# A hybrid decoder step: cached-row compression moved into sample attention, token preparation first

## The chip, the core and the metric

The kernel runs on one core of a Trainium2 chip. Its engines are TensorE (PE, with PEld for its weight loads), VectorE (DVE), ScalarE (ACT), GpSimd (POOL) and SyncE (SP, which issues the plain DMAs). The metric is device time in microseconds of one launch, as the median of the runs; less is better. All data are float32. Dense products are made from values split into a high and a low part (fp32r), in three matmuls: high x high, high weight rest x high, high x low rest.

## The reference, cut to what matters

One layer serves 512 prompt tokens and 8 sample sequences of 4 tokens each, 544 tokens in all, with the same weights. A wide projection `zin = norm(x) @ w_in` feeds three branches, and a merge and an output projection follow. The change concerns branch A (sparse attention) for the sample tokens. Each of these sequences has 2048 cached rows, in 16 pages of 128 rows; a row has the kinds k_cmp, v_cmp, k_slc, v_slc, each of 2 groups x 128 values. The rows of the first two kinds are compressed, 32 rows (16 new, 16 shared with the next block) to one, 127 blocks per sequence:

```python
blocks = jnp.concatenate([chunks[:, j:j + n_cmp] for j in range(r)], axis=2)
blocks = blocks + jnp.transpose(cmp_pe, (1, 0, 2))[:, :, None, :]
kv_c = jnp.einsum('bilcgd,clde->bicge', blocks, cmp_w.reshape(2, CMP_LEN, HEAD_DIM, HEAD_DIM))
k_c, v_c = kv_c[:, :, 0], kv_c[:, :, 1]
...
sc = jnp.einsum('bqgrd,bigd->bqgri', qb, k_c) * scale
pc = _masked_softmax(sc, (cmp_end[None, :] <= t[:, None])[None, :, None, None, :])
o_cmp = jnp.einsum('bqgri,bigd->bqgrd', pc, v_c)
imp = jnp.einsum('bqgri,ij->bqgj', pc, overlap)
```

`imp` picks the 16 blocks of 64 cached rows that the selected attention reads; the window attention reads the last 512 rows. The three results are weighted by gates and added.

## The kernel before, in words

`run` (line 1728 on) sets the order. First comes **phase_c** (L319), a stage of its own. For each of 8 sequences and 16 row positions `dma(n)` lets POOL gather a tile `pg` (128 partitions x 512 values: key and value of 128 rows) by the row numbers in `idx`; PE transposes it four times into `pT`; ACT and DVE make the high and low parts `sh` and `sl`; and `mms(n)` runs 12 matmuls of 256 columns into `cP` against the compression weights (`cwh`, `cwl`). `fin` adds the bias `peb` (the compressed `cmp_pe`) and writes keys to the DRAM tensor `kcd`; values go, transposed, to `vcd`. Beside it, as a side generator, run `params` and `x_prep` (L276): it loads five tiles of token rows (the fifth has the 32 sample tokens), squares, scales and transposes them into `hT`.

Then `open_d` splits `hT` into `hhi` and `hlo`, and **run_units** walks a list of dense units: kv, gate and q columns (84 units), two gate blocks (64), merge columns, pooling, convolution, merge columns, then the branch and output projections; 612 in all. One unit is 4 k-tiles x 3 products x 2 halves = 24 matmuls of 272 columns into `zin`. Its weights are loaded by SP into `wr` six units ahead (a load of 512 KB serves two units) and split three units ahead into `wh` and `wl`.

The rest of the work hangs on this list as generators, the `sides`: after each unit every side makes `rate` steps, a step being the code up to its next yield. The rate is 1, but 1.5 in the first merge columns (units 148 to 244) and 1.7 in the second. `kv_side` compresses the prompt's rows with weights `cw` loaded for it; `attn_p` is the prompt's attention; after it, in the same chain, comes **samp** (L1319). `samp` first reads `kcd` and `vcd` back (`load`, tiles `kc`, `vc`), makes scores `sc`, a softmax, and outputs `oc`, with lags of two steps, in ten steps for four pairs of sequences. Then `samp_group` makes window and selected attention per pair. The cached rows for it (kinds 2 and 3) are gathered by `need()`: a group is eight gathers of 128 partitions x 256 values into four `kr` tiles, and `need(1)` issues as many groups as leave `AHEAD` = 2 waiting behind the one that it returns. A scheduler orders the built program on each engine. All sides take tiles from one pool `u` of 32 SBUF buffers (`s.U`) and one of four PSUM buffers (`s.A`), so a gather waits until the tile that last had its buffer is done.

## Time and profile before

| | us |
|---|---|
| runs: median (lowest, highest) | 2618.25 (2612.72, 2618.82) |
| span of the profiled execution | 2613.4 |
| PE busy | 2527.3 |
| DVE / ACT / POOL busy | 1165.4 / 772.4 / 490.4 |

The profile is of one execution; its own time is known as its span, from the first to the last instruction, and the runs' times stand beside it. A busy PE is a union of overlapping matmuls, so the number of dense matmuls in a stretch, not the busy share, tells how far the list has come. A fp32 matmul that is no transpose has two records in the trace (512 sO for the 256 of the program).

### The profile page before, as it was taken

Reading aid. Unit: us, or ns where it says so; the run is one execution under the profiler, and the core shown is the slowest. Engines: PE = TensorE matmul, PEld = TensorE weight load, DVE = VectorE, ACT = ScalarE, POOL = GpSimd, SP = SyncE. Lnnn points to the kernel's source line nnn. Section 1 sums busy time; section 2 is a strip of 40 time slices with the busy share of each in tenths; the row PEclk is TensorE's granted clock in tenths of the full one; section 3 lists DMA queues with packets and bytes.
Section 4 is the critical chain, followed back from the end, with each engine's and each line's share of the span. In section 5 each row is a group of like instructions: output and inputs, shape, how many; then the busy total and the mean of one; then the engine's idle time right before and its main releaser. Section 6 shows DMA issues by size and latency. Waiting matters only on the chain.

```text
span 2613.4 us, 49213 instructions
## 1 busy us (share of the span) xinstructions
PE 2527.3 (97%) x20311; PEld 2398.1 (92%) x20311; DVE 1165.4 (45%) x2360; ACT 772.4 (30%) x1445; POOL 490.4 (19%) x818
## 2 busy tenths in 40 slices
PE   7889999999999879999999999999999999999999
PEld 7889999888888778789899999998999999999999
DVE  5444422856655333323323345565546444445222
ACT  4333422333333222223222222332223332223221
POOL 6556300111000117567610110000000000000000
PEclk9999999999999989999999999999999999999999
DMA  8444333352222356676743333333555664443443
GB/s 254 140 137 137 106 89 72 87 154 69 58 74 76 106 163 183 205 217 185 222 115 103 100 98 98 86 103 107 151 146 161 187 200 136 136 136 99 128 124 88
DMA packets 454688, 342.13 MB, mean 131 GB/s; under 512 B 28767, under 2 KB 402279, under 8 KB 454464
## 3 DMA queue, kind: packets, MB, share of 16 engines
q1 hardware_dynamic: 431936, 271.85, 36.5%
q0 software_dynamic: 22528, 67.13, 8.7%
q8 instruction: 160, 2.62, 0.4%
q14 instruction: 64, 0.52, 0.1%
HBM read 291.09 MB, written 48.19 MB: 130 GB/s over the span
## 4 chain that ended last, share of the span: by engine, by line
PE 84%; DMA 6%; issue 5%; DVE 2%; ACT 1%; SPq 1%; POOL 1%; DVEq 0%; ACTq 0%; POOLq 0%
PE zin L151 62%; PE cP L151 6%; PE pT L154 2%; DMA wn<-in_cache_win_dram 2%; PE O L151 1%; PE S L151 1%; PE kT L154 1%; DMA kc<-kcd 1%; PE sS L151 1%; DMA x<-in_x_prompt_dram 1%; PE sO L151 1%; PE y L151 1%; PE PT L154 1%; PE ns L151 1%; PE pm L151 0%
## 5 line engine op out<-in xcount | busy, mean ns | idle before, releaser
L151 PE MATMUL zin<-hhi,wh 128*128 128x272 f32 (+1 forms) x3616 | 783.8, 297 | 1.5 <-ACT hhi L171 0.8
L151 PE MATMUL zin<-hhi,wl 128*128 128x272 f32 (+1 forms) x3616 | 758.3, 290 | 0.0
L151 PE MATMUL zin<-hlo,wh 128*128 128x272 f32 (+1 forms) x3616 | 757.8, 291 | 0.0
L174 DVE TENSOR_TENSOR wl<-wr,wh 128x512 fp32r<-128x512 f32 (+1 forms) x612 | 422.9, 691 | 728.0 <-ACT wh L171 719.3
L171 ACT ACTIVATE wh<-wr 128x512 fp32r<-128x512 f32 (+1 forms) x612 | 383.7, 628 | 1066.2 <-PE zin L151 934.6
L151 PEld LDWEIGHTS zin<-hhi,wh 128*128 128x128 f32 (+1 forms) x3616 | 571.6, 190 | 30.9 <-issue 24.9
L151 PEld LDWEIGHTS zin<-hhi,wl 128*128 128x128 f32 (+1 forms) x3616 | 573.0, 189 | 2.8 <-issue 1.5
L151 PEld LDWEIGHTS zin<-hlo,wh 128*128 128x128 f32 (+1 forms) x3616 | 569.1, 190 | 6.1 <-issue 5.3
L313 POOL DMA_INDIRECT kr<-in_cache_kv_dram,idx x256 | 249.6, 975 | 317.9 <-DVE wl L174 193.0
L151 PE MATMUL zin<-bh,wh 128*128 128x272 f32 x1280 | 266.1, 289 | 2.7 <-DVE gt L183 2.7
L151 PE MATMUL zin<-bh,wl 128*128 128x272 f32 x1280 | 264.9, 288 | 0.0
L151 PE MATMUL zin<-bl,wh 128*128 128x272 f32 x1280 | 264.8, 288 | 0.0
L151 PEld LDWEIGHTS zin<-bh,wh 128*128 128x128 f32 x1280 | 200.5, 188 | 3.1 <-ACT wh L171 2.9
L151 PEld LDWEIGHTS zin<-bh,wl 128*128 128x128 f32 x1280 | 200.6, 188 | 0.0
L151 PEld LDWEIGHTS zin<-bl,wh 128*128 128x128 f32 x1280 | 200.5, 188 | 0.0
L151 PE MATMUL cP<-sh,cwh 128*128 128x256 f32 (+1 forms) x512 | 157.6, 308 | 3.2 <-ACT sh L171 3.2
L151 PE MATMUL cP<-sl,cwh 128*128 128x256 f32 (+1 forms) x512 | 148.3, 290 | 0.8 <-DVE sl L174 0.8
L151 PE MATMUL cP<-sh,cwl 128*128 128x256 f32 (+1 forms) x512 | 148.8, 291 | 0.0
L313 POOL DMA_INDIRECT pg<-in_cache_kv_dram,idx x128 | 124.8, 975 | 97.8 <-PE pT L154 74.6
L174 DVE TENSOR_TENSOR sl<-pT,sh 128x512 fp32r<-128x512 f32 x128 | 88.3, 690 | 108.2 <-ACT sh L171 106.1
L171 ACT ACTIVATE sh<-pT 128x512 fp32r<-128x512 f32 x128 | 76.3, 598 | 153.0 <-PE pT L154 140.7
L154 PE MATMUL pT<-cst,pg 128*128 128x128 f32 x512 | 83.1, 288 | 28.2 <-ACT junk L171 19.3
(392 smaller groups left out, 2379.2 us busy)
## 6 DMA issues: line engine op xcount, KB each, us to landing
wr<-in_w_in_dram SPq DMA_DIRECT2D x224, 512.0 KB
wr<-in_w_branch_dram SPq DMA_DIRECT2D x48, 512.0 KB
wr<-in_w_out_dram SPq DMA_DIRECT2D x32, 512.0 KB
mgd<-mg SPq DMA_DIRECT2D x48, 272.0 KB
gt<-mgd SPq DMA_DIRECT2D x48, 272.0 KB
wn<-in_cache_win_dram SPq DMA_DIRECT2D x32, 256.0 KB
out_dram<-wn SPq DMA_DIRECT2D x24, 256.0 KB
bx<-brd SPq DMA_DIRECT2D x16, 272.0 KB
```

Source lines behind the costliest of these rows:

```text
L151: return s.nc.tensor.matmul(out, l, r, start=start, stop=stop, **kw)
L154: return s.nc.tensor.transpose(out, in_, s.c("ident")[:k, :k])
L171: return s.nc.scalar.activation(out, in_, f, **kw)
L174: return (eng or s.nc.vector).tensor_tensor(out, a, b, op=op)
L313: return nc.gpsimd.indirect_dma_start(out=out, out_offset=None, in_=rows, in_offset=bass.IndirectOffsetOnAxis(ap=s.idx[kind][:, b * 16 + l ...
```

## The change

The compression stage is gone. `x_prep` and `params` run first, by themselves, and `x_prep` writes `hhi` and `hlo` straight from its transposes; the norm weights come in by four loads and are multiplied in with the scaling.

The compressed branch of the sample tokens is computed in another order (`samp_cmp`, twice, for x = 0, 1, four sequences each). For the scores, the key weights go to the queries: eight weight tiles `cw` are transposed (`wT`) and multiplied with the queries (`qw`, kept in eight `QW` tiles), and the raw cached keys, gathered and transposed (`kT`), are multiplied with these (`cS`); two shifted selections (`sel`) add the halves of a block. For the values, the probabilities are multiplied with the raw cached values (`pv`, tiles `xv`), these sums are transposed (`xvT`), and only then multiplied with the value weights (`ocT`). The bias comes from 64 matmuls with one output row in `kv_side` (`pe`). `need()` now serves four kinds: 32 groups of eight gathers for the keys and values of the compressed branch, then the 32 groups of before.

Of PE's instructions in the program go 512 `pT`, 1536 `cP`, 16 each of `sc`, `oc` and `vT`; there come 256 `kT`, 256 `cS`, 128 `pv`, 64 each of `wT`, `qw`, `xvT`, `ocT` and `pe`, and some 30 small ones. POOL's gathers go from 128 of 512 values and 256 of 256 values to 512 of 256 values. SP loses the 8 `kc`, 8 `vc`, 8 `kcd`, 8 `vcd` and 16 `wr` transfers of the compression and gains 32 `cw` loads of 256 KB. No matmul of `zin` comes or goes (14688).

```diff
-        for kind, (o, mul) in {0: ("tok2", 256.0), 2: ("tok4k", 512.0), 3: ("tok4v", 512.0)}.items():
+        pg = s.cp0.tile([128, 8], F, name="pgf")
+        s.ts(pg, p[:, :8], 512.0)
+        for kind in range(4):
             s.idx[kind] = s.cp0.tile([128, 128], U32, name=f"idx{kind}")
-            s.stt(s.idx[kind].rearrange("p (b l) -> p b l", b=8), p[:, :8, None].to_broadcast([128, 8, 16]), mul,
-                  s.c(o)[:, None, :].to_broadcast([128, 8, 16]), OP.mult, OP.add)
-        s.zf = s.cp0.tile([128, 4], F, name="zf")
-        nc.gpsimd.memset(s.zf, 0.0)
+            s.stt(s.idx[kind].rearrange("p (b l) -> p b l", b=8), pg[:, :, None].to_broadcast([128, 8, 16]),
+                  float(kind), s.c("tok4")[:, None, :].to_broadcast([128, 8, 16]), OP.add, OP.add)
...
+        def scale(i):
+            r, ss = rows(i), J.pop(i)
+            nc.vector.tensor_reduce(ss[:r, 4:5], ss[:r, :4], axis=AX.X, op=OP.add)
+            s.rsqrt(ss[:r, 5:6], ss[:r, 4:5], 1.0 / DM, ss[:r, 6:7])
...
+                s.stt(X[i][q][:r, :512], X[i][q][:r, :512], ss[:r, 5:6], W[q][:r, :512])
...
+                s.hsplit(pv, s.hhi[:, k, c], s.hlo[:, k, c])
...
-    def phase_c(s):
-        nc, a = s.nc, s.a
-        cm, cp = s.pool("cph")
...
-        def dma(n):
-            if n >= 128:
-                return
-            t = cp.tile([128, 512], F, name=s.nm("pg"), tag="pg", bufs=5)
-            s.gather(t, n // 16, n % 16, 0, 2)
-            pages[n] = t
...
-        def mms(n):
-            b, l = divmod(n, 16)
-            hi, lo = SL.pop(n)
-            if l == 0:
-                PP[b] = s.Z("cP")
-            for c in range(2):
-                n_ = 128 if b else 130
-                o = PP[b][:, c, :2 * n_].rearrange("p (g c) -> p g c", g=2)
-                wh, wl = W[c, l // 4]
-                for h2 in range(2):
-                    for m, (w_, x_) in enumerate(((wh, hi), (wl, hi), (wh, lo))):
-                        s.mm(o, w_[:, 4 * h2 + l % 4, :], x_[:, 2 * c:2 * c + 2, h2:h2 + n_],
-                             start=(l == 0 and h2 == 0 and m == 0),
-                             stop=(l == 15 and h2 == 1 and m == 2))
...
+        p, pe = s.A("pc"), s.A("pe")
+        for v, n in ((p, 128), (pe, 256)):
+            s.mm(v[:, :n], s.zb[:, :128], s.zb[:, :n], True, False, skip_group_check=True)
...
+            for c in range(2):
+                for e in range(4):
+                    l = c * 32 + 4 * j + e
+                    s.mm(pe[32 * e:32 * e + 1, c * 128:c * 128 + 128], s.pe[:, l:l + 1],
+                         w[c][:, e * 128:e * 128 + 128], False, j == 7, skip_group_check=True)
...
-        todo = [(q, kind, lq) for q in range(4) for kind in (2, 3) for lq in range(4)]
+        todo = []
+        for x in range(2):
+            todo += [(2 * x + y, 0, lq) for y in range(2) for lq in range(4)]
+            todo += [(2 * x + y, 1, lq) for lq in range(4) for y in range(2)]
+        todo += [(q, kind, lq) for q in range(4) for kind in (2, 3) for lq in range(4)]
...
-        def load(q):
-            kc, vc = s.U("kc"), s.U("vc")
-            kv_ = kc[:, :NP].rearrange("p (b g x) -> p b g x", b=2, g=2)
-            vv_ = vc[:, :NP].rearrange("p (b g x) -> p b g x", b=2, g=2)
-            for bl in range(2):
-                nc.sync.dma_start(kv_[:, bl, :, :127], s.kcd[2 * q + bl][:, :, :127])
-                nc.sync.dma_start(vv_[:127, bl], s.vcd[2 * q + bl][:127])
-            K[q] = kv_, vv_
...
+        for x in range(2):
+            yield from s.samp_cmp(x, imp, CI, need)
...
+    def cmp_w(s, c, j):
+        w = s.U("cw")
+        src = s.a["cmp_w"][0].rearrange("c (l d) e -> c l d e", l=32)
+        s.nc.sync.dma_start(w[:, :512].rearrange("p (l e) -> p l e", l=4), src[c, 4 * j:4 * j + 4].rearrange("l d e -> d l e"))
+        return w
+    def keys4(s, raw, CI, out):
+        for ci, bl, g in CI:
+            p = s.A("kT")
+            for e in range(4):
+                u, o = raw[bl, e]
+                s.tr(p[:, e * 128:e * 128 + 128], u[:, o + g * 128:o + g * 128 + 128])
+            u = s.U("kT")
...
+            out.append(u)
+            if ci % 2:
+                yield
...
+    def samp_cmp(s, x, imp, CI, need):
+        nc = s.nc
+        qv = s.qs[:, 2 * x:2 * x + 2].rearrange("p q c w -> p (q c) w")[:, :, :16]
+        sel, = s.cu("sel")
+        pgt = s.U("pgt")[:, :256].rearrange("p (y c) -> p y c", y=2)
+        QW = [s.U("QW") for _ in range(8)]
+        W = {j: s.cmp_w(0, j) for j in (0, 4)}
+        need(0)
+        yield
+        for j in range(4):
+            wt = []
+            for h in range(2):
+                w = W.pop(4 * h + j)
+                p = s.A("wT")
+                for e in range(4):
+                    s.tr(p[:, e * 128:e * 128 + 128], w[:, e * 128:e * 128 + 128])
+                u = s.U("wT")
...
+                wt.append(u)
+                if j < 3:
+                    W[4 * h + j + 1] = s.cmp_w(0, 4 * h + j + 1)
+            yield
+            for e2 in range(2):
+                p = s.A("qw")
+                for e in range(2):
+                    for h in range(2):
+                        o = (e * 2 + h) * 128
+                        c = (2 * e2 + e) * 128
+                        s.mm(p[:, o:o + 128].rearrange("p (b w) -> p b w", b=8), wt[h][:, c:c + 128], qv)
+                o = QW[2 * j + e2][:, :NP].rearrange("p (e b h w) -> p e h b w", e=2, b=8, h=2)
+                v = p.rearrange("p (e h b w) -> p e h b w", e=2, h=2, b=8)
+                for e in range(2):
...
+            yield
+        for y in range(2):
+            q = 2 * x + y
+            S = s.A("cS")
+            for lq in range(4):
+                kT = []
+                yield from s.keys4(need(), CI, kT)
+                for e in range(4):
+                    l = 4 * lq + e
+                    for ci, bl, g in CI:
+                        o = (l % 2) * 256 + (4 * y + ci) * 32
+                        s.mm(S[32 * ci:32 * ci + 32, :128], QW[l // 2][:, o:o + 32], kT[ci][:, e * 128:e * 128 + 128],
+                             l == 0, l == 15)
+            su = s.U("cS")
+            nc.vector.tensor_copy(su[:, :128], S[:, :128])
+            if y == 0:
+                p = s.A("pebT")
+                s.tr(p[:, :128], s.peb[:, :128])
+                pb = s.U("pebT")
+                s.act(pb[:, :128], p[:, :128])
+            yield
+            p = s.A("sc")
+            for h in range(2):
+                s.mm(p[:, :127], sel[:, h * 128:h * 128 + 128], su[:, h:h + 127], h == 0, False)
+            s.mm(p[:, :127], s.qs[:, q].rearrange("p c w -> p (c w)"), pb[:, :127], False, True)
+            mx, sm = s.small(1), s.small(1)
...
+            s.ts(pg[:, :129], pc[:, :129], s.gns[:, q, 0:1])
+            yield
+            p = s.A("pcT")
+            s.tr(p[:127, :128], pc[:, 1:128])
+            for h in range(2):
+                s.tr(p[:, 128 + h * 128:256 + h * 128], pg[:, 1 - h:129 - h])
...
+            s.tt(imp[r, :33], p[r, :33], s.c("forced")[r, :33], OP.add)
+        del QW
+        UT = []
+        W = {}
+        for lq in range(4):
+            xv = []
+            for y in range(2):
+                q = 2 * x + y
+                raw = need()
+                p = s.A("pv")
+                for e2 in range(2):
+                    for ci, bl, g in CI:
+                        v = raw[bl, 2 * e2][0][:, :NP].rearrange("p (l x) -> p l x", l=2)[:, :, g * 128:g * 128 + 128]
+                        s.mm(p[32 * ci:32 * ci + 32, e2 * 256:e2 * 256 + 256].rearrange("p (l d) -> p l d", l=2),
+                             pgt[:, y, 32 * ci:32 * ci + 32], v)
+                u = s.U("xv")
...
+                xv.append(u)
+                yield
+            if lq > 1:
+                W[lq - 2] = s.cmp_w(1, lq - 2)
+            for l2 in range(2):
+                p = s.A("xvT")
+                for e in range(2):
+                    for y in range(2):
+                        s.tr(p[:, (e * 2 + y) * 128:(e * 2 + y) * 128 + 128], xv[y][:, (2 * l2 + e) * 128:(2 * l2 + e) * 128 + 128])
+                u = s.U("xvT")
...
+                UT.append(u)
+            yield
+        p = s.A("ocT")
+        for j in range(8):
+            w = W.pop(j)
+            if j + 2 < 8:
+                W[j + 2] = s.cmp_w(1, j + 2)
+            for e in range(4):
+                l = 4 * (j % 4) + e
+                v = UT[l // 2][:, (l % 2) * 256:(l % 2) * 256 + 256].rearrange("p (b h w) -> p h b w", b=8, h=2)[:, j // 4]
+                s.mm(p[:, :128].rearrange("p (b w) -> p b w", b=8), w[:, e * 128:e * 128 + 128], v, j == 0 and e == 0, False,
+                     skip_group_check=True)
+            yield
...
+        nc.vector.tensor_copy(s.ocT[:, x], p[:, :128])
...
-        s.sides = [s.chain(s.params(), s.x_prep())]
-        s.drive(s.phase_c())
-        while s.sides:
-            s.step()
         s.open_d()
+        for _ in s.x_prep():
+            pass
+        for _ in s.params():
+            pass
+        s.late_consts()
```

On PE, the start of the program, before (`pT` transposes of gathered rows, `cP` the compression):

```order
L154 MATMUL pT_130<-cst,pg_106 128x128 x4
L154 MATMUL pT_143<-cst,pg_108 128x128 x4
L154 MATMUL pT_200<-cst,pg_110 128x128 x4
L154 MATMUL pT_228<-cst,pg_112 128x128 x3
L151 MATMUL cP_213<-sh_135,cwh_119 128x260
L151 MATMUL cP_213<-sh_135,cwl_120 128x260
L154 MATMUL pT_228<-cst,pg_112 128x128
```

and now (`xT` transposes of token tiles; `x_139` is the last of the third row tile, `x_141` to `x_147` are the fourth, `x_149` begins the fifth):

```order
L158 MATMUL xT_285<-cst,x_133 128x128 x4
L158 MATMUL xT_292<-cst,x_135 128x128 x4
L158 MATMUL xT_299<-cst,x_137 128x128 x4
L155 MATMUL zin_472<-hhi,wh_452 128x272
L158 MATMUL xT_306<-cst,x_139 128x128 x4
L158 MATMUL xT_334<-cst,x_141 128x128 x4
L158 MATMUL xT_341<-cst,x_143 128x128 x4
L158 MATMUL xT_348<-cst,x_145 128x128 x4
L158 MATMUL xT_355<-cst,x_147 128x128 x4
L158 MATMUL xT_374<-cst,x_149 128x32 x4
L155 MATMUL zin_472<-hhi,wh_452 128x272
```

The compression's rows are gone, and the first dense matmul stands ahead of the transposes of later tokens.

On POOL, the gathers for the compression, before (in phase_c; the CASTs fill a column of `sh` and `sl`):

```order
L313 DMA pg_1262<-in_cache_kv_dram,idx_80 128x512
L358 CAST sh_1235<-zf 128x4
L358 CAST sl_1236<-zf 128x4
L313 DMA pg_1287<-in_cache_kv_dram,idx_80 128x512
L358 CAST sh_1269<-zf 128x4
L358 CAST sl_1270<-zf 128x4
```

and now (in samp, at the end of the first half's values and the beginning of the second half's keys; `x2` is two gathers into one tile):

```order
L336 DMA kr_8505<-in_cache_kv_dram,idx_84 128x256 x2
L336 DMA kr_8508<-in_cache_kv_dram,idx_84 128x256 x2
L336 DMA kr_8511<-in_cache_kv_dram,idx_84 128x256 x2
L336 DMA kr_8514<-in_cache_kv_dram,idx_84 128x256 x2
L336 DMA kr_8574<-in_cache_kv_dram,idx_82 128x256 x2
L336 DMA kr_8577<-in_cache_kv_dram,idx_82 128x256 x2
L336 DMA kr_8580<-in_cache_kv_dram,idx_82 128x256 x2
L336 DMA kr_8583<-in_cache_kv_dram,idx_82 128x256 x2
```

The gathers follow each other without other work between them, and each brings half as many bytes.

On PE, the compressed branch, before (`kc` are compressed keys read back):

```order
L151 MATMUL zin_10175<-hlo,wh_10171 128x272 x2
L151 MATMUL sc_10339<-kc_10259,qs 32x127 x4
L151 MATMUL zin_10359<-hhi,wh_10203 128x272 x2
L151 MATMUL zin_10359<-hhi,wl_10204 128x272 x2
L151 MATMUL zin_10359<-hlo,wh_10203 128x272 x2
L151 MATMUL zin_10359<-hhi,wh_10203 128x272 x2
```

and now, at its first values (`pv`, on gathered `kr` tiles):

```order
L155 MATMUL pv_8226<-kr_7951,pgt_6842 32x256 x2
L155 MATMUL pv_8226<-kr_7957,pgt_6842 32x256 x2
L155 MATMUL pv_8226<-kr_7954,pgt_6842 32x256 x2
L155 MATMUL pv_8226<-kr_7960,pgt_6842 32x256 x2
L155 MATMUL zin_8177<-hhi,wh_8063 128x272 x2
L155 MATMUL zin_8177<-hhi,wl_8064 128x272 x2
L155 MATMUL zin_8177<-hlo,wh_8063 128x272 x2
L155 MATMUL zin_8177<-hhi,wh_8063 128x272 x2
L155 MATMUL zin_8177<-hhi,wl_8064 128x272 x2
L155 MATMUL zin_8177<-hlo,wh_8063 128x272 x2
L155 MATMUL pv_8277<-kr_8035,pgt_6842 32x256 x2
L155 MATMUL pv_8277<-kr_8041,pgt_6842 32x256 x2
```

A dense unit of 24 `zin` rows now has one group of eight `pv` in it, each on its own gathered tiles. Counting `zin` rows, `samp_cmp` stands at units 139 to 209 of the list, `samp_group` at 211 to 317; before, the compressed branch stood at 140 to 147 and the groups at 149 to 231.

## Rows read from the trace of the kernel before

**Rows 1.** page, part 1: busy time, share of the span, instructions per engine

```profile
PE 2527.3 (97%) x20311; PEld 2398.1 (92%) x20311; DVE 1165.4 (45%) x2360; ACT 772.4 (30%) x1445; POOL 490.4 (19%) x818
```

**Rows 2.** page, part 4: the chain that ended last, shares by line

```profile
PE zin L151 62%; PE cP L151 6%; PE pT L154 2%; DMA wn<-in_cache_win_dram 2%; PE O L151 1%; PE S L151 1%; PE kT L154 1%; DMA kc<-kcd 1%; PE sS L151 1%; DMA x<-in_x_prompt_dram 1%; PE sO L151 1%; PE y L151 1%; PE PT L154 1%; PE ns L151 1%; PE pm L151 0%
```

**Rows 3.** tiles cP and hhi: count, min/median/max ns, first and last start

```profile
L151 PE MATMUL cP<-sh,cwh x512: 277/285/567, 16.4 to 303.1; 128*128 128x256 f32 x149, 128*128 128x260 f32 x22
L151 PE MATMUL zin<-hhi,wh x3616: 282/288/691, 304.5 to 2113.6; 128*128 128x272 f32 x190, 128*48 128x272 f32 x1
```

**Rows 4.** chain in order of time: start, length in us, what

```profile
2129.16 292.52 PE zin L151 x2328
```

**Rows 5.** busy time by stretch, tile zin alone: PE, PEld, DVE, ACT; clock; DMA

```profile
304.00:892.00 588.00, 453.47 (x3336) 426.29 (x3337) 10.07 (x14) 28.40 (x48) 0.99 0.32 89
892.00:958.00 66.00, 38.36 (x245) 36.55 (x244) 2.14 (x3) 1.87 (x3) 0.79 0.28 81
958.00:1338.00 380.00, 274.35 (x1971) 255.00 (x1970) 0.00 (x0) 12.45 (x20) 0.98 0.67 200
1338.00:1613.00 275.00, 262.40 (x2064) 259.37 (x2062) 5.77 (x8) 13.75 (x22) 1.00 0.37 100
```

**Rows 6.** busy time by stretch, all tiles: PE, PEld, DVE, ACT, POOL; clock; DMA

```profile
892.00:958.00 66.00, 44.57 (x327) 40.46 (x326) 16.95 (x49) 10.83 (x26) 0.00 (x0) 0.79 0.28 81
```

**Rows 7.** the group of sc by line: count, busy us, mean ns, idle

```profile
L151 PE MATMUL sc<-kc,qs 128*32 128x127 f32 x32 | 4.2, 351 | 21.4 <-DMA kc<-kcd 21.4
```

**Rows 8.** timeline of POOL: start, length in us, what, idle before

```profile
988.31 0.95 POOL L313 DMA_INDIRECT kr<-in_cache_kv_dram,idx  x1 [0.30 <-issue]
989.56 0.95 POOL L313 DMA_INDIRECT kr<-in_cache_kv_dram,idx  x1 [0.30 <-issue]
```

**Rows 9.** timeline of SP's queue at the start

```profile
22.44 4.06 SPq L283 DMA_DIRECT2D x<-in_x_prompt_dram  x4
26.55 5.04 SPq L850 DMA_DIRECT2D out_dram<-in_state_pool_dram  x8
31.68 19.83 SPq L469 DMA_DIRECT2D wr<-in_w_in_dram  x6
```

**Rows 10.** groups by line, ACT and DVE: count, busy us, mean ns, idle

```profile
L171 ACT ACTIVATE junk<-x 128x512 f32<-128x512 f32 (+1 forms) x20 | 11.9, 593 | 22.4 <-DMA x<-in_x_prompt_dram 17.5 <-DMA x<-in_x_sample_dram 4.8
L174 DVE TENSOR_TENSOR sl<-pT,sh 128x512 fp32r<-128x512 f32 x128 | 88.3, 690 | 108.2 <-ACT sh L171 106.1 <-POOL sl L358 0.8 <-ACT sm L171 0.3
L183 DVE SCALAR_TENSOR_TENSOR gt<-gt,zin 128x544 f32<-128x544 f32 x32 | 23.1, 721 | 49.1 <-PE zin L151 49.1
L179 DVE TENSOR_SCALAR sm<-sm 128x1 f32<-128x1 f32 (+1 forms) x80 | 12.3, 154 | 28.5 <-ACT P L171 26.3 <-ACT pc L171 1.8
```

**Rows 11.** busy time by stretch, all tiles, GB/s last

```profile
0.00:30.00 30.00, 12.39 (x68) 10.44 (x69) 14.42 (x23) 12.55 (x15) 18.11 (x41) 0.97 0.98 296
1000.00:1100.00 100.00, 93.92 (x818) 82.91 (x817) 30.89 (x65) 28.07 (x56) 64.03 (x68) 0.97 0.65 195
```

**Rows 12.** chain in order of time, a load of four x tiles

```profile
68.36 9.28 DMA x<-in_x_prompt_dram
```

**Rows 13.** groups by line, PE: count, busy us, mean ns, idle

```profile
L151 PE MATMUL pc<-cw,kv 128*32 128x128 f32 x256 | 9.3, 280 | 0.0
L154 PE MATMUL kT<-cst,kr 128*128 128x128 f32 x256 | 32.9, 274 | 0.0
L151 PE MATMUL ns<-bm,xe 32*128 32x128 f32 x128 | 17.9, 281 | 0.0
L151 PE MATMUL sO<-kr,sP 128*32 128x128 f32 x512 | 17.3, 276 | 0.2
L154 PE MATMUL kT<-cst,wn 128*128 128x128 f32 x64 | 13.3, 310 | 13.4 <-DMA wn<-in_cache_win_dram 13.4
```

**Rows 14.** tile kr: issue ns min/median/max, and time to landing

```profile
L313 POOL DMA_INDIRECT kr<-in_cache_kv_dram,idx x256: 942/947/1462, 844.2 to 1315.4; - x128
DMA to landing us min/median/max: 2.6/3.7/6.9
```

More of the change, by code (lines that the diff above doesn't have):

```diff
@@ L225, in setup @@
         nc.vector.tensor_copy(s.pe, p[:, :64])
-        s.peb = s.cp0.tile([128, 2], F, name="peb")
         dt = lambda n, sh: s.tc.dram_tile(sh, F, name=n)
@@ L696, in kv_side @@
             yield
+        pr = s.U("pr")
+        nc.vector.tensor_copy(pr[:, :256], pe[:, :256])
+        yield
+        pe = s.A("pe")
+        s.mm(pe[:, :256], s.c("ones"), pr[:, :256])
+        s.act(s.peb, pe[:, :256])
         kcn = s.U("kcn")
-        nc.vector.tensor_copy(kcn[:64, :128], p[:64, :128])
+        for c in range(2):
+            r = slice(64 * c, 64 * c + 64)
+            s.tt(kcn[r, :128], p[r, :128], s.peb[r, c * 128:c * 128 + 128], OP.add)
         for g in range(2):
             for h in range(4):
-                src = p[64 + 32 * g:96 + 32 * g, :128]
+                src = kcn[64 + 32 * g:96 + 32 * g, :128]
                 if h % 2:
@@ L1391, in samp @@
-        for n in range(10):
-            for f, lag in ((load, 0), (score, 2), (turn, 4), (value, 6)):
-                if 0 <= n - lag < 4:
-                    f(n - lag)
-            yield
+        s.ocT = os_[:, 256:512].rearrange("p (x c) -> p x c", x=2)
+        for x in range(2):
+            yield from s.samp_cmp(x, imp, CI, need)
         for j0, j1 in ((0, 17), (17, 33)):
@@ L1451, in keyT @@
             out = []
-            for ci, bl, g in CI:
-                p = s.A("kT")
-                for e in range(4):
-                    u, o = raw[bl, e]
-                    s.tr(p[:, e * 128:e * 128 + 128], u[:, o + g * 128:o + g * 128 + 128])
-                u = s.U("kT")
-                if ci % 2:
-                    s.act(u[:, :NP], p)
-                else:
-                    nc.vector.tensor_copy(u[:, :NP], p)
-                out.append(u)
-                if ci % 2:
-                    yield
+            yield from s.keys4(raw, CI, out)
             p = s.A("sS")
```

267 lines of the change are left out of this document (104 added, 163 removed).

## The prediction

> **What bounds the kernel now.** I read the page first. PE is busy 97% of the span and no other engine passes 45% [rows 1]; of the chain that ended last, the dense zin matmuls alone are 62% [rows 2]. So time is what PE does, plus the places where it waits. Where PE's time lies comes next: the compression stage (tiles pT and cP) runs from the start to 303.1 us, and the first zin follows at 304.5 [rows 3]. Behind it I count in units, 24 zin matmuls each. In one unbroken stretch 2328 of them take 292.52 us [rows 4], so a unit is 24 x 292.52 / 2328 = 3.02 us. The zin counts by stretch, divided by 24, give 139 units by 892 us, 10 more by 958, 82 more by 1338, 86 more by 1613 [rows 5]. Sample attention lies in these: its compressed branch at units 140 to 147, its four groups at units 149 to 231. Two weak spots show. From 892 to 958 PE is busy 44.57 of 66 us at a granted clock of 0.79 [rows 6]; sc waits 21.4 us there for loads of kc [rows 7]. And gathers (kr) leave POOL one per 1.25 us, with POOL idle 0.30 us between them for nothing but the issue: 988.31, 989.56 [rows 8]. That second number decides this case.
>
> **Term 1, the head: -256.5 us.** Phase C leaves PE's order altogether; what the dense units wait for is then x_prep alone. I work its end out twice. By loads: four x tiles take SP 4.06 us and eight state copies 5.04 [rows 9], so 20 x and 4 norm-weight loads from 1.7 us on end at 26, the copies at 31, and the first weight (six in 19.83, 3.3 each) is issued by 35 and has landed by about 38. The order puts the first zin ahead of the transposes of the later tokens, so these wait for that weight. Behind it DVE still owes the fourth and fifth row tiles: scaling 8 x 0.68 (721 ns for 544 columns, 512 here), lows 4 x 0.69 and 4 x 0.25, some ten small steps of 0.154, one weight low [rows 10], 12 us in all: 50. By DVE alone: the first tile is squared by about 10 (1.45 MB at 296 GB/s [rows 11], then 4 squares of 0.593 plus their read), and DVE's work on five tiles and three weights is 34 us: 44. I take 48. Below it, 40 if loads and DVE overlap better; above it, 60 if row tiles come as slowly as beside phase C, where four x loads took 9.28 us [rows 12]. 304.5 - 48 = 256.5.
>
> **Term 2, small: +5 us.** kv_side adds 64 matmuls with one output row for the bias. Nearest row: pc, 256 records (two per matmul) in 9.3 us [rows 13], so 64 cost 4.6. The shared x scaling and the fewer splits on ACT and DVE are off PE's path and cost nothing while zin covers them.
>
> **Term 3, sample compression: units 139 to 211 now.** By the order, its first PE row stands at unit 139, its last at 209, and the sample groups move to 211 to 317. Side work per half x, priced by rows 13: wT 32 transposes at 32.9/256 = 0.129 us and qw 32 matmuls at 17.9/64 = 0.28 make 13.1; 128 kT transposes 16.5; 128 cS at 17.3/256 = 0.068, 8.7; 64 pv, twice as wide, 8.6; xvT 4.1; ocT at most 9; softmax and the rest 3. Together 63, so 126 for both, and 72 units are 217: PE alone needs 343 us.
> But each step takes a group of eight gathers, 32 groups in this stretch, and eight issues are 10.0 us. Per group, PE needs in the key part 1.3 units and 3.1 of side work, 7 us; in the value part 1 unit and 1.6, 4.6 us. Both are under 10. POOL runs ahead only as far as buffers are free: by the order the 4th group's buffers are released at unit 146, the 19th group's at unit 178; those between come free in time. The tally:
> - unit 139 to 146: 7 x 3.02 + 11.5 = 32.6;
> - groups 4 to 16: 13 x 10.0 + 3.7 to land [rows 14] = 133.7, at unit 168 (PE alone would be there after 107);
> - to unit 178: 10 x 3.02, ocT 9, half of wT 6.5, a value step 1 = 46.7, POOL idle at its end;
> - groups 19 to 32: 14 x 10.0 + 3.7 = 143.7, at unit 203 (PE alone 122);
> - to unit 211: 24.2 + 9 = 33.2.
> Sum 390. The waits, 27 and 22 us, fall into the last five value steps of each half, some 5 us in each, and the 0.79 of rows 6 says that such waits cost clock too. At half clock a value step takes 9.2 us, still under 10.0, so only the return to full clock shows: I add 10. Stretch 400.
> The Trainium skill (TensorE: Matmul & The Clock Gate, HAM oscillation) says that a loop which waits for a DMA in each round drops to half clock in each round and pays for it every time. Rows 6 agree as far as they go (0.79 in the stretch with the kc waits). By that rule the tally stays as it is, since half clock hides under POOL's 10.0 us; only if the rule held between the waits as well would the third rival come.
>
> **Term 4, units 211 to 317.** 106 x 3.02 = 320. The groups' side work and waits in 958 to 1338 are 380 - 82 x 3.02 = 132 [rows 5]; of these 13.4 were waits for wn [rows 13], which a slower pace (one step per unit behind unit 244, not 1.5) should mostly spare: 119. The pooling branch in 1338 to 1613 leaves 275 - 86 x 3.02 = 15. Sum 454. Here a group needs over 10 us of PE, so POOL is hidden.
> Units 139 to 317 took 721 us before (892 to 1613) and take 854: **+133**. In that the kc waits are gone. SP loses eight kc loads and gains 32 cw loads, of the kind that kv_side already hides. Units behind 317 are the same.
>
> **Sum.** -256.5 + 5 + 133 = -118.5. The profiled span is 2613.4, so 2495; the median of the runs is 2618.25, 4.9 above it. **2500 us.**
>
> **Rivals.**
> - *The gathers are hidden.* PE alone sets the stretch, 343 and no clock loss: 2500 - 57 = 2443. For it: POOL is free long before unit 139. Against it: every spacing in rows 8 is 1.25 us, and buffers stop POOL from running further ahead.
> - *The gathers come slower.* 68 POOL instructions per 100 us at 1000 to 1100 [rows 11] is one per 1.47 us, the pace with buffer waits: 27 groups x 8 x 0.22 = 48 more, 2548; if each group's landing adds up too, 27 x 3.7 = 100 more, 2600. For it: the buffers for a group are often released two or three steps before it is used. The Trainium skill (SBUF - State Buffer, SBUF: two separate sides) says that descriptors for such gathers can't be written while DVE runs some operations. The 256 issues here last 942 to 1462 ns, the median 947 [rows 14], so this trace doesn't bear it out.
> - *Slower than before: the clock stays down.* If PE ran at half clock through units 139 to 211, its 343 us would be 686, 286 more than I count: 2786. It decides at 400 + 118 = 518 us, a mean granted clock of 343 / 518 = 0.66 there. For it: 0.79 with PE busy two thirds. Against it: the key part and the ocT and wT parts leave PE no long waits, and 958 to 1338, with waits of several us, kept 0.98 [rows 5].
>
> **How the numbers follow.** Forecast (2465 to 2535): 0.58. Hidden gathers: 0.10. Slower gathers: 0.27. Clock: 0.04, and 0.01 for no change, where head and stretch would each miss by 60 us. The range takes the forecast with the head's bounds, 2443 below, and the greater part of the slower gathers: 2440 to 2570. A measurement of this kernel tells 0.3%, 8 us, from no change. Faster 0.95, same 0.01, slower 0.04.
>
> **What would show it.** Right: first zin near 48 us; kr issues 1.25 us apart without a break through most of the value parts; pv as the PE group with the most idle time, waiting for the gathers, some 50 us in all; no kc wait; last soT at about 1480 us. Wrong: pv without waits (first rival), kr spacing above 1.4 us (second), PEclk of 0.6 or less over 200 us (third), or a zin start behind 60 us.

## The result and the profile after

| | us | ratio to before, 95% interval |
|---|---|---|
| before, median of 4 runs | 2616.41 | |
| changed kernel, median of 4 runs (lowest, highest) | 2503.32 (2499.2, 2504.62) | 0.9562 [0.9547, 0.9577] |
| span of its profiled execution | 2502.9 | |

The 2618.25 us in the table of before is the median of three runs; with the fourth, 2614.58, it is the 2616.41 above.

The page of the changed kernel, parts 1 and 2 (busy time and share of the span; then 40 equal slices, busy tenths and the granted clock in tenths):

```profile
PE 2403.6 (96%) x19761; PEld 2253.5 (90%) x19761; DVE 1088.8 (44%) x2217; ACT 725.0 (29%) x1380; POOL 559.6 (22%) x665
PE   4999999999997997999999899999999999999999
PEclk8999999999998998999999999999999999999999
```

Four slices show where PE is not full: the first (the head), the 13th and 16th, at 7, with the clock at 8 (751 to 813 and 939 to 1001 us), and the 23rd, at 8 (1377 to 1439 us, in units 211 to 317). Counted in units of 24 zin matmuls, as the prediction did, the time divides so:

| stretch | before | forecast | after | after - forecast |
|---|---|---|---|---|
| start to unit 84 | 608.2 | 356.7 | 365.5 | +8.8 |
| units 84 to 139 | 283.9 | 283.9 | 283.1 | -0.8 |
| units 139 to 211 | 354.4 | 400 | 395.6 | -4.4 |
| units 211 to 317 | 366.7 | 454 | 462.0 | +8.0 |
| unit 317 to the end | 1000.2 | 1000.2 | 996.7 | -3.5 |
| span | 2613.4 | 2494.8 | 2502.9 | +8.1 |

The forecast of the first row is 48 + 303.7 (units 0 to 84 before) + 5. What a reader can check of it: the timeline of PE at the start (start, length, what, how often, idle time before and its releaser):

```profile
33.58 0.57 PE L155 MATMUL zin<-hhi,wh 128*128 128x272 f32 x1
33.95 0.99 PE L158 MATMUL xT<-cst,x 128*128 128x128 f32 x4
41.89 3.44 PE L158 MATMUL xT<-cst,x 128*128 128x128 f32 x16 [6.95 <-DVE x L187]
48.31 0.53 PE L158 MATMUL xT<-cst,x 32*128 32x32 f32 x4 [2.98 <-DVE x L187]
49.21 0.59 PE L155 MATMUL zin<-hhi,wh 128*128 128x272 f32 x1 [0.37 <-ACT hhi L175]
```

One zin matmul runs at 33.58, and behind it PE stands in its own order before the transposes of the fourth and fifth row tiles, which wait 6.95 and 2.98 us for DVE's scaling. The dense work begins at 49.2. Tile zin alone in the two long stretches (busy time and count of PE, PEld, DVE, ACT; clock; DMA share; GB/s), the answer to [rows 5]:

```profile
648.60:1044.20 395.60, 247.11 (x1728) 230.37 (x1728) 2.15 (x3) 11.25 (x18) 0.94 0.58 170
1044.20:1506.20 462.00, 348.33 (x2544) 326.15 (x2544) 5.74 (x8) 16.79 (x27) 0.99 0.60 177
```

1728 matmuls are the 72 units of the first, 2544 the 106 units of the second. In the first the granted clock is 0.94; all tiles together, for the stretch and for its two value parts:

```profile
648.60:1044.20 395.60, 359.54 (x3189) 326.55 (x3186) 110.70 (x202) 95.62 (x177) 249.28 (x268) 0.94 0.58 170
742.00:815.00 73.00, 56.18 (x447) 44.57 (x444) 14.69 (x29) 13.25 (x24) 55.48 (x62) 0.87 0.60 175
916.00:1011.00 95.00, 76.18 (x679) 63.46 (x677) 21.94 (x39) 18.80 (x34) 72.90 (x77) 0.89 0.56 163
```

In the value parts PE is busy 56.18 of 73 and 76.18 of 95 us and the clock is 0.87 and 0.89. What it waits for stands in the groups by line (count, busy us, mean ns, idle and its releaser):

```profile
L155 PE MATMUL pv<-kr,pgt 128*32 128x256 f32 x256 | 29.1, 431 | 35.2 <-DMA kr<-in_cache_kv_dram,idx 35.2
L158 PE MATMUL kT<-cst,wn 128*128 128x128 f32 x64 | 10.6, 296 | 4.1 <-DMA wn<-in_cache_win_dram 4.1
```

pv waits 35.2 us for gathers; wn, 13.4 us in [rows 13], has 4.1. The timeline of POOL in the first value part, beside [rows 8]:

```profile
786.02 0.95 POOL L336 DMA_INDIRECT kr<-in_cache_kv_dram,idx  x1 [0.30 <-issue]
787.27 0.94 POOL L336 DMA_INDIRECT kr<-in_cache_kv_dram,idx  x1 [0.30 <-issue]
788.52 0.95 POOL L336 DMA_INDIRECT kr<-in_cache_kv_dram,idx  x1 [0.30 <-issue]
789.77 0.95 POOL L336 DMA_INDIRECT kr<-in_cache_kv_dram,idx  x1 [0.30 <-PE pv L155]
```

and all gathers of the changed kernel (issue ns: lowest, median, highest; first and last start):

```profile
L336 POOL DMA_INDIRECT kr<-in_cache_kv_dram,idx x512: 940/946/1667, 604.4 to 1481.8; - x171
```

The issues follow each other at 1.25 us. Averaged over the fourth to the seventeenth group behind the first (688 to 829 us) it is 1.273, over groups 19 to 31 (871 to 1008) 1.325: the 103 steps between its 104 issues take 7.8 us more than 103 x 1.25, 3.7 of them because some issues last a few hundred ns longer and 4.1 because POOL waits once, 4.31 us ahead of 885.25, for a buffer. Between the two, 27.7 us pass from one issue to the next: the pause that the tally had at units 168 to 178.

### The profile page after: what moved, and what is told of

The parts are those of the page before. It is cut to its first block, busy times and chain, and to the rows that moved or that the text cites. A ratio compares the mean times of both kernels' runs of the same rounds, so it can differ in the third digit from the quotient of the medians.

```text
span 2502.9 us, 47446 instructions
## 1 busy us (share of the span) xinstructions
PE 2403.6 (96%) x19761; PEld 2253.5 (90%) x19761; DVE 1088.8 (44%) x2217; ACT 725.0 (29%) x1380; POOL 559.6 (22%) x665
## 5 line engine op out<-in xcount | busy, mean ns | idle before, releaser
L336 POOL DMA_INDIRECT kr<-in_cache_kv_dram,idx x512 | 503.4, 983 | 492.7 <-PE PT L158 197.1
L1307 DVE COPY kT<-kT 128x512 f32<-128x512 f32 x72 | 49.5, 689 | 91.0 <-PE kT L158 87.4
L158 PE MATMUL kT<-cst,kr 128*128 128x128 f32 x512 | 69.0, 277 | 0.0
L158 PEld LDWEIGHTS kT<-cst,kr 128*128 128x128 f32 x512 | 56.5, 140 | 7.8 <-issue 5.5
L155 PE MATMUL pv<-kr,pgt 128*32 128x256 f32 x256 | 29.1, 431 | 35.2 <-DMA kr<-in_cache_kv_dram,idx 35.2
L175 ACT ACTIVATE mg<-zin 128x544 f32<-128x544 f32 x48 | 29.9, 622 | 109.3 <-PE zin L155 109.3
L175 ACT ACTIVATE P<-S,sm 128x512 f32<-128x512 f32 (+3 forms) x64 | 33.8, 528 | 86.7 <-DVE sm L184 84.4
L175 ACT ACTIVATE kT<-kT 128x512 f32<-128x512 f32 x72 | 43.0, 597 | 53.8 <-PE kT L158 52.1
```

The lines of the kernel that those rows point to most:

```text
L155: return s.nc.tensor.matmul(out, l, r, start=start, stop=stop, **kw)
L158: return s.nc.tensor.transpose(out, in_, s.c("ident")[:k, :k])
L175: return s.nc.scalar.activation(out, in_, f, **kw)
L336: return nc.gpsimd.indirect_dma_start(out=out, out_offset=None, in_=rows, in_offset=bass.IndirectOffsetOnAxis(ap=s.idx[kind][:, b * 16 + l ...
L1307: s.nc.vector.tensor_copy(u[:, :NP], p)
```

## The experiments

The theory: in the compressed branch POOL's issue pace sets the time, eight issues of 1.25 us a group, and PE's waits are what is left of that behind PE's own work. The rivals: bytes, landing or the release of buffers set it; or the waits can't be won back. Each line of the table is the median of a kernel's runs (four each, two of slow_issues and of no_phase_c) beside the runs of before on the same chip; "139 to 420" is the time from unit 139 to unit 420 in the trace, behind which all samples' work is done. Before has 1124.9 there. With more yields less of the sample work falls into units 139 to 211 (3013 records of PE in slow_values, 3189 in the changed kernel), so those kernels compare with the others by 139 to 420 alone.

| kernel | median us | ratio, 95% interval | pv waits us | 139 to 211 | 139 to 420 |
|---|---|---|---|---|---|
| changed kernel | 2503.32 | 0.9562 [0.9547, 0.9577] | 35.2 | 395.6 | 1260.1 |
| after_again | 2507.44 | 0.9588 [0.9572, 0.9604] | 35.1 | 396.0 | 1261.0 |
| half_issues | 2456.16 | 0.9388 [0.9373, 0.9404] | 0.0 | 338.8 | 1204.8 |
| slow_issues | 2541.40 | 0.9707 [0.9688, 0.9726] | 42.2 | 426.9 | 1293.3 |
| slow_values | 2464.29 | 0.9400 [0.9377, 0.9423] | 0.0 | 322.7 | 1222.1 |
| slow_values_1b | 2491.56 | 0.9524 [0.9509, 0.9540] | 17.5 | 356.2 | 1249.9 |
| slow_values_half_b | 2463.25 | 0.9438 [0.9404, 0.9471] | 0.0 | 322.7 | 1215.8 |
| slow_values_pace_b | 2469.30 | 0.9447 [0.9426, 0.9467] | 0.0 | 322.6 | 1227.6 |
| no_phase_c | 2368.79 | 0.9048 [0.9030, 0.9066] | | 353.1 | 1125.8 |

### Half the issues, the same bytes

```diff
-                        s.gather(u[:, (e % 2) * 256:(e % 2) * 256 + 256], 2 * q + bl, lq * 4 + e, kind)
+                        if kind > 1:
+                            s.gather(u[:, (e % 2) * 256:(e % 2) * 256 + 256], 2 * q + bl, lq * 4 + e, kind)
+                        elif e % 2 == 0:
+                            s.gather2(u[:, :512], 2 * q + bl, lq * 4 + e)
```

> Leaves out half of the compressed branch's cached rows: one gather of 512 values (key and value of a row) fills a tile that two gathers of 256 values filled, so a group of the compressed branch has 4 POOL issues, not 8; bytes, tiles, buffers and all PE work are the same. Theory (POOL's issue pace sets the value parts): an issue still takes about 1.25 us, a group 5 us, less than PE needs for a step, so the idle time before pv falls from 35.2 us to under 8, the granted clock of the stretch is 0.97 or more, units 139 to 211 take about 345 us in place of 395.6, and the run about 2453 us (2440 to 2465). Rival (bytes, landing or the release of buffers set the pace): nothing of that changes, 395 us in the stretch, 2495 to 2510 us.

Measured: 2456.16 us, 47 less. All tiles in units 139 to 211, then the group of pv, then two of the gathers of 512 values:

```profile
653.90:992.70 338.80, 338.02 (x3189) 314.41 (x3187) 110.23 (x202) 95.61 (x177) 133.17 (x148) 1.00 0.67 199
```

```profile
L155 PE MATMUL pv<-kr,pgt 128*32 128x256 f32 x256 | 17.1, 385 | 0.0
```

```profile
768.98 0.94 POOL L348 DMA_INDIRECT kr<-in_cache_kv_dram,idxp  x1 [0.30 <-issue]
770.23 0.95 POOL L348 DMA_INDIRECT kr<-in_cache_kv_dram,idxp  x1 [0.30 <-PE xvT L158]
```

A gather of twice the bytes is issued in the same 0.94 us and 1.25 us behind the last. With four of them a group no wait for a gather is left, PE is busy 338.02 of 338.8 us, and the clock is 1.00. The rival falls: bytes and buffers are unchanged, and a landing is no shorter (3.8 us in the median, 3.7 in [rows 14]). The rows are halved with the issues; that POOL's issuing sets the pace, and not the rows on their way, slow_issues shows below. The same 3189 PE records were busy 359.54 us in the changed kernel: 21.5 us of its 56.8 more are clock, 35.2 the waits. The stretch without waits is also near the 343 us that the prediction had for PE alone. The run shows 47 and not 57 us because its set-up of a second index table costs 5.3 us before unit 139 and some 2 to 5 us differ from run to run elsewhere.

### Slower issues

```diff
+                        if kind < 2:
+                            nc.gpsimd.memset(u[:, (e % 2) * 256:(e % 2) * 256 + 256], 0.0)
                         s.gather(u[:, (e % 2) * 256:(e % 2) * 256 + 256], 2 * q + bl, lq * 4 + e, kind)
```

> POOL clears each tile's half with a memset before the gather that fills it, in the compressed branch's 32 groups alone; nothing else changes. A memset of this size and what orders it should add 0.3 to 0.6 us to each of the 256 issues. Theory (issue pace): 27 of the 32 groups are issued back to back, so the stretch grows by 27 x 8 x 0.3 to 0.6 = 65 to 130 us, nearly all of it in idle time before pv (and later kT), and the run takes 2570 to 2635 us. Rival (bytes, landing or buffers): POOL has time to spare, the run stays within 2495 to 2515 us.

Measured: 2541.40 us, 38 more: the direction of the theory, under its lower end of 65, in neither range. POOL's timeline shows why:

```profile
782.93 0.58 POOL L1263 MEMSET kr<- 128x256 f32 x2
783.66 0.95 POOL L336 DMA_INDIRECT kr<-in_cache_kv_dram,idx  x1 [0.16 <-POOL kr L1263]
784.92 0.94 POOL L336 DMA_INDIRECT kr<-in_cache_kv_dram,idx  x1 [0.30 <-issue]
785.86 0.58 POOL L1263 MEMSET kr<- 128x256 f32 x2
```

Two memsets run as a pair of 0.58 us ahead of two gathers, and take the place of 0.30 us of idle time: two issues take 2.94 us in place of 2.5. Over groups 4 to 17 (counted from 0) the mean spacing is 1.502, 0.23 more than 1.273, not 0.3 to 0.6. By 0.23 the first half's last value group (number 15) should be issued 12 x 8 x 0.23 = 22 us later, and it is: its last gather at 831 us, not 809. Of these 22 us 13 arrive at unit 178: the compiled order has more dense units ahead of the last pv steps here, and POOL's pause behind group 17 shrinks from 27.7 to 15 us, so group 18 starts only 13 us later. The second half adds 18. So the dose reached PE, but a part of it went into the pause: 31 us in the stretch, with pv's waits

```profile
L155 PE MATMUL pv<-kr,pgt 128*32 128x256 f32 x256 | 32.3, 445 | 42.2 <-DMA kr<-in_cache_kv_dram,idx 42.2
```

only 7 us longer, and 13.3 us of new waits before pcT (the transposed probabilities). These are not waits for late keys. The softmax ahead of pcT waits for a small memset of `pc` on POOL, which stands behind the slowed gathers in POOL's own order:

```profile
759.46 0.60 DVE L183 TENSOR_SCALAR pc<-pc,sm 128x129 f32<-128x129 f32 x1 [5.01 <-POOL pc L1384]
```

The second half has the same with 8.55 us. So POOL's pace reaches PE here by a second path beside the gathers.

### More dense work in the value steps

```diff
                 xv.append(u)
                 yield
+                yield
+                yield
```

> Two more yields behind each pv step, so that a value step has 2.3 dense units on PE in place of 1; same work, same gathers, same order of all else. Theory (PE waits for gathers in the value parts only because it comes too early): the samples' groups move about 21 units down the list, the idle time before pv falls from 35.2 us to under 5, the granted clock of the stretch is 0.97 or more, and the run takes 2503 - 35 to 60 = 2443 to 2468 us. Rival (the gain is given back: the sample groups then meet the pooling branch's work or the second merge's pace, or their own gathers wait): 2490 to 2510 us.

Measured: 2464.29 us, 39 less, with the whole computation done: the fastest such kernel here, 0.9400 of before. The group of pv, that of scT (part of the state-space branch), and all tiles in units 139 to 211:

```profile
L155 PE MATMUL pv<-kr,pgt 128*32 128x256 f32 x256 | 17.3, 385 | 0.0
L158 PE MATMUL scT<-cst,cc 128*27 128x128 f32 x12 | 3.5, 292 | 6.9 <-POOL cc L887 6.8
```

```profile
650.80:973.50 322.70, 322.26 (x3013) 302.13 (x3011) 98.60 (x183) 92.25 (x171) 204.28 (x223) 1.00 0.61 180
```

No wait for a gather, clock 1.00. But of the 55.3 us that half_issues won between units 139 and 420 it won 38.0, so 17.3 went elsewhere; scT shows 6.9 us of wait for POOL (idle in the changed kernel: 0.1). The sample groups moved by 32 units, not 21: soT, their last transpose, comes at unit 349, in the changed kernel at 317. Three runs were to tell where the 17.3 us went. On the first chip PE had long waits for nothing that the profile shows (last section), so there they decide nothing. Their expectations were

> Both edits at once: two more yields behind each pv step, and half of the compressed branch's cached rows left out by gathers of 512 values (4 POOL issues a group). Question: why slow_values won 39 us where half_issues won 47 with 5 us of extra set-up in it. Theory A (moving the sample groups 21 units down the list costs something itself: scT, soT and wn waits and PE at a lower granted clock, seen in slow_values from 1050 to 1550 us): here too, 2466 to 2476 us, above half_issues' 2456. Theory B (what was left in slow_values is still POOL's issue pace): the move is free, 2448 to 2460 us.

> One more yield behind each pv step, not two: the groups move some 11 units, not 21. Theory A (the move costs something itself, the waits for gathers as well): pv keeps under 12 us of waits, less is lost behind unit 244, 2455 to 2470 us, within 6 us of slow_values' 2464. Theory B (only the waits for gathers count): 2470 to 2485 us, as two yields take the waits away and one does not.

> Two more yields behind each pv step, and the pace of 1.5 steps per unit kept for 20 units more (to 264), so that the sample groups end nearly where they ended before the move. Theory A (what slow_values lost lies in the sample groups meeting the work behind unit 317): 2448 to 2460 us. Rival (it lies in the groups' own waits or in gathers that meet other POOL work, whatever the pace): 2460 to 2475 us.

There the runs gave 2591.89, 2724.47 and 2734.36 us beside 2768.88 for before. All three ran again on one other chip, with the changed kernel as a control:

> The changed kernel, unaltered, as a control beside the three that follow: the chip of the last runs showed 118 to 131 us of issue gaps on PE while gathers ran, which no earlier run had. Without such gaps: 2503 us (2496 to 2511), ratio 0.953 to 0.959. With them, more than 2700 us.

It gave 2507.44 us, with the same waits and spacing as the first profile (1.274 and 1.323 us).

> Two more yields behind each pv step, and half of the compressed branch's cached rows left out by gathers of 512 values, measured again. Theory A (moving the sample groups 21 units costs something itself): 2466 to 2476 us. Theory B (what was left in slow_values was POOL's pace): 2448 to 2460 us.

It gave 2463.25 us, just under what theory A said and above B's range, with set-up as in half_issues. Between units 139 and 420 it needs 1215.8 us, 11.0 more than half_issues: so much the move of the sample groups costs by itself, with no pv waiting for a gather:

```profile
L155 PE MATMUL pv<-kr,pgt 128*32 128x256 f32 x256 | 17.2, 385 | 0.0
L158 PE MATMUL scT<-cst,cc 128*27 128x128 f32 x12 | 3.6, 303 | 6.4 <-POOL cc L899 6.3
```

scT waits 6.4 us there (0.1 in half_issues), nearly all for POOL; as pm waits less (5.4 us against 10.2), PE is idle 5.0 us more in all and busy 6.0 us longer. The other 6.3 of the 17.3 us come with the full number of gathers, without a wait for one: theory A holds for about two thirds, B for at most a third.

> One more yield behind each pv step, measured again. Theory A (the move of the sample groups costs something itself, the waits for gathers as well): pv keeps under 12 us of waits, less is lost behind unit 244, 2455 to 2470 us on a chip without the issue gaps. Theory B (only the waits for gathers count): 2470 to 2485.

It gave 2491.56 us, over both ranges. One yield took away half of the waits, where theory A asked for under 12 us:

```profile
L155 PE MATMUL pv<-kr,pgt 128*32 128x256 f32 x256 | 23.9, 397 | 17.5 <-DMA kr<-in_cache_kv_dram,idx 17.5
```

and won 10.2 us between units 139 and 420, where two yields won 38.0. Where waits are left, what PE gains by half of the way is small: 17.7 us less waiting gave 10 (by the medians, against the control, 15.9).

> Two more yields behind each pv step and the pace of 1.5 kept until unit 264, measured again. Theory A (what slow_values lost lies in the sample groups meeting the work behind unit 317): 2448 to 2460 us. Rival (it lies in the groups' own waits or in gathers that meet other POOL work, whatever the pace): 2460 to 2475 us.

It gave 2469.30 us, in the range of the rival; against slow_values' 0.9400 its ratio of 0.9447 is no gain. At the faster pace the pooling branch's pm waits for ACT:

```profile
L155 PE MATMUL pm<-plh,pwh 128*128 128x272 f32 x32 | 10.4, 344 | 16.8 <-ACT pwh L175 16.8
```

where slow_values has 7.0; scT's 6.9 us of waits are gone in exchange (0.1). But the last soT comes at unit 339, against 349 in slow_values and 317 in the changed kernel, so the pace took back only 10 of the 32 units. The run shows that this pace wins nothing on balance; what the groups cost behind unit 317 stays open.

### The head alone

```diff
-        s.drive(s.phase_c())
+        nc.gpsimd.memset(s.peb, 0.0)
...
-                nc.sync.dma_start(kv_[:, bl, :, :127], s.kcd[2 * q + bl][:, :, :127])
-                nc.sync.dma_start(vv_[:127, bl], s.vcd[2 * q + bl][:127])
+                nc.sync.dma_start(kv_[:, bl, :, :127], a["cache_win"][0, 2 * q + bl][:128, 0, :, :127])
+                nc.sync.dma_start(vv_[:127, bl], a["cache_win"][0, 2 * q + bl][:127, 1])
```

> The kernel before without its compression stage: phase C is left out, its bias is zero, and the compressed branch reads its keys and values from another input, with the same loads. x_prep and open_d are those of before, run by themselves. Theory (the head costs what the loads, squares, scalings and transposes of the tokens cost, 256 us less than with phase C): first zin at 45 to 70 us (its x_prep has more steps than the new one), units behind it as before, 2355 to 2385 us. Then the change's new compression costs what is between this and 2503 us, 120 to 150. Rival (phase C had covered work that the dense units then carry, or the units at the start run slower without it): 2390 us or more.

Measured: 2368.79 us, in the range of the theory: 249.8 us less than before (2618.60 on that chip). Tile hhi (count, lowest, median and highest ns, first and last start):

```profile
L151 PE MATMUL zin<-hhi,wh x3616: 283/288/694, 49.6 to 1868.9; 128*128 128x272 f32 x190, 128*48 128x272 f32 x1
```

The first dense matmul at 49.6, with x_prep as it was: the new x_prep begins its dense work at 49.2, so the rewrite of x_prep gained nothing there, and the head's gain is phase C's absence alone. The changed kernel lies 134.5 us above this one: the price of the compression in its new place, with its bias, less the waits for kc that it spares (sc still waits 21.0 us here).

## Why the prediction was right

**Term 1, the head (-256.5): mechanism right, 7 to 9 us too much** (no_phase_c saves 249.8 us; the first row of the table above misses by 8.8). The dense work starts at 49.2 against 48, and what it waits for last is what was named: DVE's scaling of the fourth and fifth tiles ahead of PE's transposes. The steps up to there had other sizes, so the nearness is in part luck. The first zin ran at 33.58, where its weight was to land at about 38; from there to 49.21 it took 15.6 us, not 12, and in these DVE stands 2.24 us for a load of constants that the prediction didn't count:

```profile
38.65 0.23 DVE L265 CAST trib<-cu 128x128 bf16<-128x128 f32 x1 [2.24 <-DMA cu<-in_cst_u_dram]
```

The step that failed is that units 0 to 84 were taken to run as before. All tiles in units 0 to 24 and 24 to 84, first without phase C, then before:

```profile
49.60:128.40 78.80, 77.72 (x588) 75.42 (x589) 30.05 (x56) 26.72 (x46) 0.00 (x0) 0.95 0.28 74
128.40:362.90 234.50, 231.53 (x1940) 214.13 (x1939) 117.00 (x197) 67.86 (x121) 20.49 (x32) 0.96 0.36 99
```

```profile
304.50:379.40 74.90, 74.90 (x590) 72.91 (x591) 28.54 (x47) 28.20 (x49) 0.00 (x0) 1.00 0.34 91
379.40:608.20 228.80, 227.05 (x1941) 210.95 (x1940) 116.83 (x197) 69.73 (x122) 20.51 (x32) 0.99 0.37 101
```

With the same work on the list behind the head, 9.6 us more without phase C (313.3 against 303.7 us): the same 1940 records of units 24 to 84 are busy 231.53 in place of 227.05 us at 0.96 in place of 0.99, and the first 24 units run at 0.95, not 1.00. In the timeline of PE above, the head leaves PE idle 10 of the last 14 us before 49. Past unit 24 the clock of the changed kernel stands at its lower level twice (0.50 from 263.4 to 273.7 and from 321.5 to 324.9 us), behind waits of PE of 0.93 and 1.09 us. In slow_values_pace_b, the same kernel up to unit 139, waits of 0.94 and 1.08 us left it at 1.00, and unit 84 came at 359.4 us; in the eight traces of kernels alike up to there it comes at 359.4 to 367.8. So a part of the miss differs from one execution to the next, and what decides it no run here settles.

**Term 2, the bias (+5).** The records of pe:

```profile
L155 PE MATMUL pe<-cw,peT x128: 270/273/421, 313.4 to 343.9; 128*1 128x128 f32 x128
```

128 of them, 6.5 us busy by the groups of lines; units 0 to 84 take 3.0 us more than in no_phase_c (316.3 against 313.3), whose x_prep differs too. Both are near 5; with 8.4 us between traces of the same code at unit 84, no run here measures the term closer.

**Term 3, the compression (400): right, and its tally almost point by point.** Unit 139 to 168 had 32.6 + 133.7 = 166.3 us and took 166.4; to 178, 46.7 and 46.3; to 203, 143.7 and 150.2; to 211, 33.2 and 32.7. The sum of 390 came to 395.6. PE alone was put at 343 and is 338.8. The waits were put at 27 + 22 in the last value steps of each half: they fall there, but only 35.2 us of them are idle time; the rest of the 56.8 us between the two stretches is PE at a lower clock. That half clock would hide under POOL's 10.0 us is what the tally up to unit 168 bears out: 166.4 us with PE at 0.94, as counted for full clock. The 10 us set aside for the return of the clock weren't needed; 6.5 us came instead behind unit 178, from the spacing of groups 19 to 31, 1.325 and not 1.25 (13 x 8 x 0.075 = 7.8): half of it one wait for a buffer, half longer issues. So the stretch was right by a term that was mis-named.

The Trainium skill (TensorE: Matmul & The Clock Gate, HAM oscillation) says that a loop which waits for a DMA each round falls to half clock round after round. The two value parts agree as far as rows go (0.87 and 0.89, and 1.00 in half_issues and slow_values, where no gather is waited for), though not with every wait: in each the clock fell three times, for 6.8 to 10.2 us, over four or five steps that wait. Its price showed only in part, since eight issues took longer than PE's step even so.

At the second rival the prediction misread its rows: it took the issues of [rows 14] for undisturbed by DVE because their median is 947 ns. 28 of those 256 last over 0.97 us, and 24 of the 28 begin while DVE subtracts two tiles in SBUF (last section). The price is small here: in groups 4 to 17 longer issues add 2.1 us, in groups 19 to 31 3.7. The Trainium skill (SBUF - State Buffer, SBUF: two separate sides) says that a DVE operation with two inputs in SBUF holds up a GpSimd operation that reads SBUF until it has ended. The traces agree: a gather reads its `idx` there, and a late issue ends 0.82 us behind the subtraction in the median.

**Term 4, units 211 to 317 (454).** It took 462.0, and 461.8 in half_issues: no wait for a gather is behind the 8 us. wn waits fell from 13.4 to 4.1, as the prediction had it. PE is idle 16.4 us, 9.7 of them before pm, which waits for ACT; in before those waits were 0.8 us at this place. The prediction took the pooling branch's 15 us over as they were, and didn't ask what it waits for when the sample groups run beside it: that is the term's miss.

**The sum.** The errors of the terms, +8.8, -0.8, -4.4, +8.0 and -3.5, leave 8.1 us in the span. The 4.9 us from span to median, taken over from before, were 0.4 here (and 3.0 in before, by the median of its four runs), so that 2500 stands against 2503.32. The nearness is owed in part to that. Of the signs, pv's waits are 35.2 us and not some 50, as told above, and the last soT comes at 1505.8, not 1480; the sum itself has unit 317 at 2494.8 - 1000.2 = 1494.6.

**The rivals.** Hidden gathers: 2443 was said for a kernel without waits, and half_issues with 5.3 us of set-up gave 2456; POOL's spacing in the changed kernel speaks against the rival, as the prediction said. Slower gathers: the spacing was 1.27 and 1.33, not 1.47; slow_issues shows what 1.50 costs, 38 us against the 48 worked out. (With each landing added on top, 48 and 100 make 2648, not 2600.) The clock staying down: 0.94 in the stretch, far above the 0.66 from which it would decide. No change: no.

## What to carry to other kernels

When work moves from a stage of its own under other work, count the slowest queue that it uses, in issues and not in bytes, against the time that the cover has per step: here eight gathers of 1.25 us stood against 4.6 to 7 us of PE, by the prediction's estimate. Pace the consumer to that queue: two more dense units' worth in a value step won 39 us with nothing else changed, and half of that remedy won less than half (10 of 38 us between units 139 and 420). What moves later in the list then meets other side work on the same engines (scT's on POOL; in the changed kernel pm's on ACT); with half the issues that took back 11 of the 55 us that were to be had.

## What was not expected of the hardware

An issue of a gather costs the same 0.94 us, and 1.25 us from one to the next, for 128 rows of 512 values as for 128 rows of 256 (half_issues, above): the price is by row or by issue, which no run here tells apart.

An issue that begins while DVE subtracts (`wl`, the low part of a weight, from two tiles in SBUF) lasts longer. DVE's and POOL's timelines in the changed kernel:

```profile
734.90 0.69 DVE L178 TENSOR_TENSOR wl<-wr,wh 128x512 fp32r<-128x512 f32 x1 [2.73 <-ACT wh L175]
735.03 1.38 POOL L336 DMA_INDIRECT kr<-in_cache_kv_dram,idx  x1 [0.30 <-issue]
```

Of the 512 issues 75 begin in such a subtraction; 59 of these last over 0.97 us, and 57 of the 59 end 0.81 to 0.86 us behind the subtraction. Of the 329 that begin while DVE runs nothing, 3 last that long; of the 34 that begin while DVE copies kT from PSUM, 1 does. In the kernel before it is 24 of the 31 that begin in a subtraction and 1 of the 162 that begin while DVE runs nothing.

On one chip every kernel was slower, the traced ones only while gathers ran (behind unit 420 slow_values_1 took 593.0 us there, slow_values_1b 593.8). Its three runs have 73.0, 131.4 and 118.2 us of PE idle time that the profile puts down to issue, in gaps of 0.4 us in the median and of up to 3.4, those above 0.2 us all between 619 and 1780 us, where gathers run; every other run here has at most 0.1 us of it. The kernel with half of the compressed branch's issues lost least (0.9358 of before there; the others 0.9825 and 0.9865). A piece of PE's timeline and the group of one matmul in slow_values_1 on that chip:

```profile
709.87 0.39 PE L155 MATMUL zin<-hhi,wh 128*128 128x272 f32 x1 [0.20 <-issue]
711.30 0.39 PE L155 MATMUL zin<-hhi,wh 128*128 128x272 f32 x1 [1.04 <-issue]
711.49 0.66 PE L155 MATMUL zin<-hhi,wl 128*128 128x272 f32 x2
712.73 0.39 PE L155 MATMUL zin<-hlo,wh 128*128 128x272 f32 x1 [0.59 <-issue]
```

```profile
L155 PE MATMUL zin<-hlo,wh 128*128 128x272 f32 (+1 forms) x3616 | 779.6, 296 | 37.3 <-issue 36.9
```

Here dense matmuls, in the middle of a unit, wait for nothing that the profile shows. What holds PE's instructions back on that chip, and whether the gathers or something beside the kernel does it, stays open; before took 2768.88 us there and 2614.84 to 2618.60 on the other chips, which is why the ratios from that chip are compared with no others.
